# One-core hybrid decoder layer: contiguous halves for the modulation and Q/K weights, and a reordered start

## The chip, the cores and the metric

The kernel runs on one core of one Trainium2 chip. The metric is the device time of one execution, in microseconds (us). Lower is better. Everything is float32 outside; large products are split into a rounded high part and a low remainder, so that three fast passes replace one slow float32 product.

## The reference, cut to what matters

One decoder layer over 256 tokens of width 1024, with a modulation computed from a single vector `c`:

```
mod   = silu(c) @ w_ada + b_ada            # 3 x 1024
shift, scale, gate = split(mod, 3)
h     = rmsnorm(x, norm_g) * (1 + scale) + shift
proj  = h @ w_in                           # ten blocks of 1024 columns: q, k, v, ...
attn  = causal softmax attention(q, k, v) + relative-position bias
y     = two gated branches (attention, short convolution), merged
out   = rmsnorm(x + gate * (merged @ w_out), final_g)
```

With 256 tokens there is one key block, so the attention is plain causal attention with the bias `rel_bias[bucket(distance)]` for each head. This case is about what happens before and in the first projection: `silu(c)`, the two modulation columns `shift` and `scale` for each of eight 128-row slices of `h`, the normalized and transposed input, the bias table, and then `q` and `k`.

## The kernel before

The work is staged as: prologue, Q/K projection, V projection, 36 column units (convolution, gates, merges, the attention heads woven between them), output projection, tail. The order of most of the prologue is fixed by hand: `pin` keeps an instruction in program order on its engine. Every engine runs its own list in order.

**Loads.** SyncE (SP) issues nearly all loads, in the order of the code: the vector `c` into row 96 of a zeroed tile `crow` (L123), the two halves of `x` (L124, L125), the modulation weights of slice 0 in two pieces (`load_ada`, L103), the first Q/K slab in two halves (`load_slab`, L114), then the small table `oneh` for the bias (L129), then slice by slice a modulation tile (`load_wide`, L108) and a slab. Each modulation tile and each slab is 128 rows of 2048 numbers, 1 MB; every load takes 1024 of the 2048 columns, so in DRAM its rows are 4 KB long and start 8 KB apart. ScalarE (ACT) issues one load at the start, `vecs` (L122).

**Prologue.** TensorE runs four warm-up products (L231), then the broadcast of `c` over 128 partitions in two halves of 512 columns (`broadcast`, L237: a product of ones with the 97 rows of `crow`, 96 of them zero), the transposition of `vecs` between them (L249), one warm-up product, the eight transposed and normalized blocks of the first token half (`xn_trans(0, k, d0)`, L228), one warm-up, the eight of the second half, the product that picks the bias values out of `oneh` (L272), two warm-ups, and then the first Q/K slice (`passes(0)`, L221: sixteen float32 products, 32 records).

Beside it ACT squares and sums both halves of `x` (`square`, L246; the first before the sigmoid of the first half of `c`), applies the sigmoid (L242), and builds the diagonal matrices `d0`, `d1` from the reciprocal roots that GpSimd (POOL) computes (`rms_diag`). VectorE (DVE) finishes `silu(c)` (L243) and forms the modulation dots: for slice 0 four dots of 512 columns (`ada_dot`, L165), each into its own column of `parts`, which a reduction (L168) adds to the bias that POOL copied into a fifth column (L263). The first modulated slice `hfs[0]` (L275) on ACT waits for that sum, and `passes(0)` for `hfs[0]`.

**Q/K loop.** For each slice i (L286): DVE computes the modulation of the next slice in two dots of 1024 columns (`wide_dot`, L173, which start from the bias), ACT and DVE split the next slab into high and low parts (L203, L210), ACT and DVE make the next slice of `h` (L181, L191), and TensorE accumulates 16 column tiles into all eight PSUM banks (L221). After the loop comes V, whose products need nothing from the prologue but `h`.

Of the kernel before, what the change touches and what calls it, by code (L numbers as in the profile page):

```python
# [26 lines left out]
WARM = 4  # L27
WARM2 = 1
WARM3 = 1
WARM4 = 2  # L30
CROW = 96
HALF = 8
AHEAD = 3
VCUT = 640
NATIVES = [16, 2, 0, 0, 0, 0, 0, 0]
CUTS0 = (0, 2, 4)
UNITS = ([("ada", i) for i in range(KT)] + [("gate", i) for i in range(4)]
# [7 lines left out]
def layer_kernel(ctx: ExitStack, tc, x, c, vec, wp_all, slab_all, onehot, final_g, out):  # L45
# [48 lines left out]
    scs = const.tile([P, KT, 2], F32, name="scs")  # L94
    parts = const.tile([P, KT, 2, 5], F32, name="parts")
# [4 lines left out]
    def load_ada(i, cuts):  # L100
        adas[i] = big.tile([P, 2048], F32, tag=("AT", "YB", "V")[i % 3], name=f"ada{i}")
        for a, b in zip(cuts, cuts[1:]):
            pin(nc.sync.dma_start(adas[i][:, a * 512:b * 512], wp_all[UNIT["ada", i]][:, a * 512:b * 512]))  # L103

    def load_wide(i):
        adas[i] = big.tile([P, 2048], F32, tag=("AT", "YB", "V")[i % 3], name=f"ada{i}")
        for s in range(2):
            pin(nc.sync.dma_start(adas[i][:, s * D:(s + 1) * D], wp_all[UNIT["ada", i]][:, s * D:(s + 1) * D]))  # L108

    def load_slab(i, h):  # L110
        if h == 0:
            slabs[i] = raw_tile([P, NT * P], f"slab{i}")
        cols = slice(HALF * P, NT * P) if h else slice(0, HALF * P)
        pin(nc.sync.dma_start(slabs[i][:, cols], slab_all[i * P:(i + 1) * P, cols]))  # L114

    def load_ktile(i):
        load_slab(i, 0)
        if i + 1 < KT:
            load_wide(i + 1)
        load_slab(i, 1)  # L120

    pin(nc.scalar.dma_start(vecs, vec))  # L122
    pin(nc.sync.dma_start(crow[CROW:CROW + 1, :], c))  # L123
    pin(nc.sync.dma_start(xx[:, 0, :], x[0:P, :]))  # L124
    pin(nc.sync.dma_start(xx[:, 1, :], x[P:2 * P, :]))  # L125
    load_ada(0, CUTS0)
    for h in range(2):
        load_slab(0, h)
    pin(nc.sync.dma_start(oneh, onehot))  # L129
    load_wide(1)  # L130
    for i in range(1, AHEAD):
# [4 lines left out]
    nc.vector.memset(mhalf, -0.5)  # L136
    nc.vector.memset(parts[:, :, :, 2:4], 0.0)
    make_identity(nc, ident)
# [18 lines left out]

    def ada_dot(i, cuts, n):
        for a, b in zip(cuts, cuts[1:]):
            w = (b - a) * 256  # L160
            for s in range(2):
                for q in range(0, w, n):
                    k = a * 256 + q
                    src = adas[i][:, a * 512 + s * w + q:a * 512 + s * w + q + n]
                    pin(nc.vector.tensor_tensor_reduce(src, src, csb[:, k:k + n], vT[:, i:i + 1] if s else 1.0, 0.0,  # L165
                                                       ALU.mult, ALU.add, parts[:, i, s, k // n:k // n + 1]))
                    yield
        pin(nc.vector.reduce_sum(scs[:, i, :], parts[:, i], axis=mybir.AxisListType.X))  # L168

    def wide_dot(i):  # L170
        for s in range(2):
            src = adas[i][:, s * D:(s + 1) * D]
            pin(nc.vector.tensor_tensor_reduce(src, src, csb, vT[:, i:i + 1] if s else 1.0, modb[:, i, s:s + 1],  # L173
                                               ALU.mult, ALU.add, scs[:, i, s:s + 1]))

    def run(gen, n=9):
        for _ in range(n):
            next(gen, None)

# [64 lines left out]

    def square(t):
        pin(nc.scalar.activation(xx[:, 2 + t, :], xx[:, t, :], AF.Square, accum_out=ss[:, t:t + 1]))  # L246
# [12 lines left out]
    d1 = rms_diag(ss[:, 1:2], "r1")  # L259
    modb = vT[:, 8:24].rearrange("p (k s) -> p k s", s=2)  # L260
    pin(nc.gpsimd.tensor_scalar_add(modb[:, :, 1], modb[:, :, 1], 1.0))
    pin(nc.gpsimd.tensor_mul(modb[:, :, 1], modb[:, :, 1], vT[:, 0:KT]))
    pin(nc.gpsimd.tensor_copy(parts[:, :, :, 4], modb))  # L263
# [373 lines left out]


def _ada(w, cols, cuts):
    t = [w[:, c0:c0 + P].T for c0 in cols]  # L640
    return np.concatenate([h[:, a * 256:b * 256] for a, b in zip(cuts, cuts[1:]) for h in t], axis=1)


def _layout(inp):
    w_ada, w_in = inp["w_ada"][0], inp["w_in"][0]
    w_o = {"oa": inp["w_o_attn"][0], "oc": inp["w_o_conv"][0]}
    units = []
    for key in UNITS:
        blk = key[0]
        if blk == "ada":  # L650
            units.append(_ada(w_ada, [key[1] * P, D + key[1] * P], (0, 4) if key[1] else CUTS0))
        elif blk == "gate":
            units.append(_ada(w_ada, [2 * D + (2 * key[1] + d) * P for d in range(2)], (0, 4)))
# [11 lines left out]
    return {"x": inp["x"], "c": inp["c"], "vec": vec, "wp": np.stack(units), "slab": w_in[:, 0:NT * P],  # L665
            "onehot": np.concatenate([_onehot(), inp["rel_bias"]], axis=1), "final_g": inp["final_g"]}
# [17 lines left out]
```

## Time and profile before

| what | value |
|---|---|
| median of three runs | 330.81 us |
| the three runs | 330.81, 330.83, 327.39 us |
| the profiled execution's own time | 327.31 us |
| its span in the trace | 325.5 us |
| TensorE busy | 317.4 us |
| VectorE busy | 247.2 us |
| ScalarE busy | 187.8 us |
| DRAM read | 71.39 MB |

The span runs from the first to the last instruction of the trace; the execution's own time has 1.8 us more around it. Busy times are sums of instruction times; a float32 product appears as two records on TensorE. Times in the rows are microseconds from the start of the span, unless a column says ns.

### The profile page before, as it was taken

Reading aid. Unit: us, or ns where it says so; the run is one execution under the profiler, and the core shown is the slowest. Engines: PE = TensorE matmul, PEld = TensorE weight load, DVE = VectorE, ACT = ScalarE, POOL = GpSimd, SP = SyncE. Lnnn points to the kernel's source line nnn. Section 1 sums busy time; section 2 is a strip of 40 time slices with the busy share of each in tenths; the row PEclk is TensorE's granted clock in tenths of the full one; section 3 lists DMA queues with packets and bytes.
Section 4 is the critical chain, followed back from the end, with each engine's and each line's share of the span. In section 5 each row is a group of like instructions: output and inputs, shape, how many; then the busy total and the mean of one; then the engine's idle time right before and its main releaser. Section 6 shows DMA issues by size and latency. Waiting matters only on the chain.

```text
span 325.5 us, 4909 instructions
## 1 busy us (share of the span) xinstructions
PE 317.4 (98%) x1894; PEld 280.5 (86%) x1894; DVE 247.2 (76%) x406; ACT 187.8 (58%) x304; POOL 6.4 (2%) x18
## 2 busy tenths in 40 slices
PE   8899999999999999999999999999999999999992
PEld 5799999988888888888888888888888888888892
DVE  1889985874469777796857998999755566888764
ACT  6255646745498586775757656766565636453430
POOL 2300000000000000000000000000000000000010
PEclk9999999999999999999999999999999999999999
DMA  6999999985474345434533559559974656400003
GB/s 223 388 408 410 406 413 416 393 322 222 156 250 139 131 186 197 136 130 158 200 159 131 224 204 375 222 155 408 366 283 172 265 178 221 157 3 0 0 2 129
DMA packets 14175, 72.77 MB, mean 224 GB/s; under 512 B 1503, under 2 KB 2887, under 8 KB 8008
## 3 DMA queue, kind: packets, MB, share of 16 engines
q1 hardware_dynamic: 12562, 70.45, 57.1%
q10 hardware_dynamic: 1558, 2.00, 1.8%
q8 instruction: 15, 0.25, 0.3%
q14 instruction: 8, 0.07, 0.1%
q0 software_dynamic: 32, 0.01, 0.0%
HBM read 71.39 MB, written 1.06 MB: 223 GB/s over the span
## 4 chain that ended last, share of the span: by engine, by line
PE 92%; DMA 3%; issue 1%; SPq 1%; ACT 0%; DVE 0%; POOL 0%; POOLq 0%; ACTq 0%
PE acc L221 15%; PE aoa L349 5%; PE aoc L349 5%; PE acx L349 5%; PE acc L349 5%; PE acb L349 5%; PE ama L349 5%; PE amc L349 5%; PE aga L349 5%; PE agc L349 5%; DMA oneh<-in_onehot_dram 3%; PE aoa L350 2%; PE aoc L350 2%; PE acx L350 2%; PE acb L350 2%; PE acc L350 2%
## 5 line engine op out<-in xcount | busy, mean ns | idle before, releaser
L173 DVE CUSTOM_DVE_ANT_0 ada<-ada,csb,vT 128x1024 f32<-128x1024 f32 x14 | 17.8, 1309 | 0.0
L416 DVE CUSTOM_DVE_ANT_0 L<-pS,BI 128x128 f32<-128x128 f32 x8 | 2.3, 292 | 12.2 <-PE pS L413 12.2
L221 PE MATMUL acc<-hf,slab 128*128 128x256 f32 x36 | 8.1, 379 | 0.0
L581 POOL TENSOR_TENSOR rf<-ms,mhalf 128x1 f32<-128x1 f32 x2 | 1.7, 866 | 303.8 <-DVE ms L606 300.2
L221 PEld LDWEIGHTS acc<-hf,slab 128*128 128x128 f32 x36 | 6.7, 190 | 0.8
L563 ACT ACTIVATE SQ<-TT 128x512 f32<-128x512 f32 x3 | 1.9, 627 | 7.6 <-DVE TT L558 7.6
L386 DVE CUSTOM_DVE_ANT_0 gate<-gate,csb,vT 128x512 f32<-128x512 f32 x8 | 6.0, 746 | 0.2 <-DMA gate<-in_wp_dram 0.2
L349 PE MATMUL acc<-H,cc2h 128*128 128x512 f32 x16 | 5.8, 404 | 0.0
L349 PE MATMUL aoa<-GA,oa0h 128*128 128x512 f32 x16 | 5.8, 404 | 0.0
L349 PE MATMUL aoa<-GA,oa1h 128*128 128x512 f32 x16 | 5.7, 399 | 0.0
L349 PE MATMUL aoc<-GC,oc2h 128*128 128x512 f32 x16 | 5.7, 399 | 0.0
L349 PE MATMUL aoc<-GC,oc1h 128*128 128x512 f32 x16 | 5.7, 399 | 0.0
L349 PE MATMUL aoa<-GA,oa3h 128*128 128x512 f32 x16 | 5.7, 399 | 0.0
L349 PE MATMUL acx<-H,cx0h 128*128 128x512 f32 x16 | 5.7, 398 | 0.0
L349 PE MATMUL acb<-H,cb1h 128*128 128x512 f32 x16 | 5.7, 398 | 0.0
L349 PE MATMUL aoc<-GC,oc0h 128*128 128x512 f32 x16 | 5.7, 398 | 0.0
L349 PE MATMUL aoa<-GA,oa2h 128*128 128x512 f32 x16 | 5.7, 398 | 0.0
L349 PE MATMUL aoc<-GC,oc3h 128*128 128x512 f32 x16 | 5.7, 398 | 0.0
L349 PE MATMUL acc<-H,cc0h 128*128 128x512 f32 x16 | 5.7, 398 | 0.0
L349 PE MATMUL acx<-H,cx1h 128*128 128x512 f32 x16 | 5.7, 398 | 0.0
L349 PE MATMUL acx<-H,cx3h 128*128 128x512 f32 x16 | 5.7, 398 | 0.0
L349 PE MATMUL acb<-H,cb3h 128*128 128x512 f32 x16 | 5.7, 398 | 0.0
(465 smaller groups left out, 1215.8 us busy)
## 6 DMA issues: line engine op xcount, KB each, us to landing
ada<-in_wp_dram SPq DMA_DIRECT2D x16, 512.0 KB, 9.9
slab<-in_slab_dram SPq DMA_DIRECT2D x16, 512.0 KB, 10.2
wv<-in_wp_dram SPq DMA_DIRECT2D x4, 1024.0 KB, 11.3
wcc<-in_wp_dram SPq DMA_DIRECT2D x4, 1024.0 KB, 7.8
wcx<-in_wp_dram SPq DMA_DIRECT2D x4, 1024.0 KB, 4.7
wcb<-in_wp_dram SPq DMA_DIRECT2D x4, 1024.0 KB, 5.0
wgc<-in_wp_dram SPq DMA_DIRECT2D x4, 1024.0 KB, 4.8
wga<-in_wp_dram SPq DMA_DIRECT2D x4, 1024.0 KB, 4.8
```

What stands on the lines that cost most here:

```text
L173: pin(nc.vector.tensor_tensor_reduce(src, src, csb, vT[:, i:i + 1] if s else 1.0, modb[:, i, s:s + 1], ALU.mult, ALU.add, scs[:, i, s:s + 1]))
L221: pin(nc.tensor.matmul(acc[j // 2][:, (j % 2) * S:(j % 2 + 1) * S], w[i][:, j * P:(j + 1) * P], x, start=(i == 0 and j // 2 not in opened) ...
L349: nc.tensor.matmul(a, hi[:, k, cols], rhs[:, k, :], start=(k == 0), stop=False)
L350: nc.tensor.matmul(a[:, S:], lo[:, k, cols], rhs[:, k, 0:S], start=False, stop=(k == KT - 1))
L386: nc.vector.tensor_tensor_reduce(src, src, csb[:, q * 512:(q + 1) * 512], 1.0, 0.0 if q else vT[:, 24 + b:25 + b], ALU.mult, ALU.add, gpar ...
L416: nc.vector.tensor_tensor_reduce(L[:, 0:P], pS[:, 0:P], BI[:, h, 0:P][:, ::-1], 1.0, -3.0e38, ALU.add, ALU.max, mx[:, 0:1])
L563: nc.scalar.activation(SQ[:, t, 0:w], TT[:, t, cols], AF.Square, accum_out=s8[:, slot:slot + 1])
L581: nc.gpsimd.tensor_tensor(r, ms, mhalf, op=ALU.pow)
```

## The change

1. **Layout.** On the host, each modulation tile is stored as two contiguous halves of 128 x 1024 (`_halves`), and the slabs as sixteen such blocks. A load now reads 512 KB that lie together, 128 rows of 4 KB one after the other. What lands in which tile is the same.
2. **Bias table.** `oneh` is loaded on ACT's queue right after `vecs`, not on SP's queue behind the first slab. Its product moves on TensorE from behind the transposes to right behind the second broadcast.
3. **c.** It goes into row 127 of `crow`; the broadcast has 128 rows instead of 97.
4. **First square.** The sum of squares of the first token half moves from ACT to DVE, as a product with a running sum over 1024 columns, ahead of the first `silu` product. On ACT the square of the second half now stands ahead of `d0`.
5. **Dots.** The dots of slice 0 start from the bias (or from the first half's sum), so `parts`, its memset, the reduction and POOL's copy go. The scaled bias is written into a tile of its own, `msc`, by POOL ahead of `r1`.
6. **Warm-ups.** Three instead of one ahead of the first transposes, one behind the last instead of one between the two groups, and the two behind the bias product go.

```diff
-WARM2 = 1
+WARM2 = 3
 WARM3 = 1
-WARM4 = 2
-CROW = 96
+CROW = P - 1
...
+    def load_ada(i):
         adas[i] = big.tile([P, 2048], F32, tag=("AT", "YB", "V")[i % 3], name=f"ada{i}")
+        unit = wp_all[UNIT["ada", i]]
         for s in range(2):
-            pin(nc.sync.dma_start(adas[i][:, s * D:(s + 1) * D], wp_all[UNIT["ada", i]][:, s * D:(s + 1) * D]))
+            src = bass.AP(tensor=unit.tensor, offset=unit.offset + s * P * D, ap=[[D, P], [1, D]])
+            pin(nc.sync.dma_start(adas[i][:, s * D:(s + 1) * D], src))
...
-        pin(nc.sync.dma_start(slabs[i][:, cols], slab_all[i * P:(i + 1) * P, cols]))
+        pin(nc.sync.dma_start(slabs[i][:, cols], slab_all[(2 * i + h) * P:(2 * i + h + 1) * P, :]))
...
     pin(nc.scalar.dma_start(vecs, vec))
+    pin(nc.scalar.dma_start(oneh, onehot))
...
-    pin(nc.sync.dma_start(oneh, onehot))
...
+    def first_dots(a):
+        cols = slice(a * 512, (a + 1) * 512)
+        for s in range(2):
+            src = adas[0][:, a * D + s * 512:a * D + (s + 1) * 512]
+            pin(nc.vector.tensor_tensor_reduce(src, src, csb[:, cols], vT[:, 0:1] if s else 1.0,
+                                               half[:, s:s + 1] if a else bias(0, s), ALU.mult, ALU.add,
+                                               scs[:, 0, s:s + 1] if a else half[:, s:s + 1]))
...
     broadcast(1)
-    square(0)
+    pb = pv[0:NH, P:512]
+    pin(nc.tensor.matmul(pb[:, 126:], oneh[:, 3 * P:], oneh[:, 126:3 * P], start=True, stop=True))
+    pin(nc.vector.tensor_tensor_reduce(xx[:, 2, :], xx[:, 0, :], xx[:, 0, :], 1.0, 0.0, ALU.mult, ALU.add, ss[:, 0:1]))
     silu_part(0)
     pin(nc.scalar.activation(vT, pv[:, 0:56], AF.Copy))
+    pin(nc.scalar.activation(xx[:, 3, :], xx[:, 1, :], AF.Square, accum_out=ss[:, 1:2]))
     d0 = rms_diag(ss[:, 0:1], "r0")
-    square(1)
-    dot = ada_dot(0, CUTS0, 512)
-    run(dot, 2)
+    modb = vT[:, 8:24].rearrange("p (k s) -> p k s", s=2)
+    pin(nc.gpsimd.tensor_scalar_add(msc, modb[:, :, 1], 1.0))
+    pin(nc.gpsimd.tensor_mul(msc, msc, vT[:, 0:KT]))
+    first_dots(0)
     silu_part(1)
     d1 = rms_diag(ss[:, 1:2], "r1")
...
-    run(dot)
+    first_dots(1)
     warm(WARM2)
-    for k in range(KT):
-        xn_trans(0, k, d0)
+    for t, d in enumerate((d0, d1)):
+        for k in range(KT):
+            xn_trans(t, k, d)
     warm(WARM3)
-    for k in range(KT):
-        xn_trans(1, k, d1)
-    pb = pv[0:NH, P:512]
-    pin(nc.tensor.matmul(pb[:, 126:], oneh[:, 3 * P:], oneh[:, 126:3 * P], start=True, stop=True))
-    warm(WARM4)
...
+def _halves(w):
+    return w.reshape(P, 2, D).transpose(1, 0, 2).reshape(P, 2048)
...
-    "slab": w_in[:, 0:NT * P],
+    "slab": w_in[:, 0:NT * P].reshape(KT, P, 2, D).transpose(0, 2, 1, 3).reshape(2 * KT * P, D),
```

## Rows read from the trace of the kernel before

**Rows 1.** The page: span, and busy time of each engine with its share and instructions.

```profile
span 325.5 us, 4909 instructions
...
PE 317.4 (98%) x1894; PEld 280.5 (86%) x1894; DVE 247.2 (76%) x406; ACT 187.8 (58%) x304; POOL 6.4 (2%) x18
```

**Rows 2.** Chain that ended last, in order: start us, us, what; prologue and Q/K.

```profile
4.06 9.44 DMA oneh<-in_onehot_dram
13.54 0.60 PE pv L272 x2
14.14 0.64 PE wt L147 x4
14.78 47.36 PE acc L221 x366
```

**Rows 3.** Windows: stretch, length, busy (records) by engine, granted clock, DMA share, GB/s.

```profile
3.00:4.80 1.80, 1.80 (x4) 0.29 (x3) 0.00 (x0) 0.49 (x1) 0.00 (x0) 1.00 1.03 412
5.00:10.00 5.00, 5.00 (x18) 3.92 (x18) 1.40 (x4) 3.38 (x9) 2.57 (x7) 1.00 0.86 276
...
15.00:62.00 47.00, 47.00 (x366) 46.09 (x366) 39.53 (x55) 26.70 (x35) 0.63 (x1) 1.00 1.02 409
62.00:313.00 251.00, 251.00 (x1426) 218.60 (x1425) 194.56 (x316) 152.12 (x251) 0.00 (x0) 1.00 0.52 191
```

**Rows 4.** Timeline of TensorE: start us, us, instruction, idle before and releaser.

```profile
2.92 1.92 PE L237 MATMUL pc<-crow,ones 97*128 97x512 f32 x2
...
5.04 2.07 PE L237 MATMUL pc<-crow,ones 97*128 97x512 f32 x2
6.91 0.63 PE L147 MATMUL wt<-ones 128*128 128x128 f32 x2
7.34 3.31 PE L228 MATMUL px<-r0d,xx 128*128 128x128 f32 x16
...
10.70 1.95 PE L228 MATMUL px<-r1d,xx 128*128 128x128 f32 x16
13.54 0.60 PE L272 MATMUL pv<-oneh 32*8 32x258 f32 x2 [0.89 <-DMA oneh<-in_onehot_dram]
...
14.62 7.07 PE L221 MATMUL acc<-hf,slab 128*128 128x256 f32 x32
21.34 0.83 PE L221 MATMUL acc<-H,slab1h 128*128 128x256 f32 x4
```

**Rows 5.** Tile px: ns min/median/max of one record, first and last start.

```profile
L228 PE MATMUL px<-r0d,xx x16: 275/421/421, 7.3 to 10.4; 128*128 128x128 f32 x16
...
L228 PE MATMUL px<-r1d,xx x16: 275/275/275, 10.7 to 12.4; 128*128 128x128 f32 x16
```

**Rows 6.** Timeline of the other engines beside the prologue.

```profile
0.73 0.63 ACTq L122 DMA_DIRECT2D vecs<-in_vec_dram  x1
...
4.31 1.06 ACT L246 ACTIVATE xx<-xx 128x1024 f32<-128x1024 f32 x1 [1.42 <-DMA xx<-in_x_dram]
...
6.41 0.40 ACT L155 ACTIVATE r0d<-ident,r0r 128x128 f32<-128x128 f32 x1 [0.36 <-POOL r0r L153]
...
9.28 0.69 DVE L165 CUSTOM_DVE_ANT_0 ada<-ada,csb 128x512 f32<-128x512 f32 x1 [2.62 <-DMA ada<-in_wp_dram]
...
10.57 0.68 DVE L243 TENSOR_TENSOR csb<-csb,pc 128x512 f32<-128x512 f32 x1
...
11.91 0.75 DVE L165 CUSTOM_DVE_ANT_0 ada<-ada,csb,vT 128x512 f32<-128x512 f32 x1
...
12.77 0.16 DVE L168 TENSOR_REDUCE scs<-parts 128x2 f32<-128x10 f32 x1
...
13.03 0.56 ACT L275 ACTIVATE hf<-px,scs 128x256 f32<-128x256 f32 x1 [3.83 <-DVE scs L168]
...
14.97 1.28 DVE L173 CUSTOM_DVE_ANT_0 ada<-ada,csb,vT 128x1024 f32<-128x1024 f32 x1
...
18.16 0.59 ACT L181 ACTIVATE H<-xnT,scs 128x256 fp32r<-128x256 f32 x1
```

More of the change, by code (lines that the diff above doesn't have):

```diff
@@ L35 @@
 NATIVES = [16, 2, 0, 0, 0, 0, 0, 0]
-CUTS0 = (0, 2, 4)
 UNITS = ([("ada", i) for i in range(KT)] + [("gate", i) for i in range(4)]
@@ L94, in layer_kernel @@
     scs = const.tile([P, KT, 2], F32, name="scs")
-    parts = const.tile([P, KT, 2, 5], F32, name="parts")
+    half = const.tile([P, 2], F32, name="half")
+    msc = const.tile([P, KT], F32, name="msc")
     gcol = const.tile([P, KT], F32, name="gcol")
@@ L98, in layer_kernel @@
     adas, slabs, hfs, his, los = {}, {}, {}, {}, {}
-    def load_ada(i, cuts):
+    def load_ada(i):
         adas[i] = big.tile([P, 2048], F32, tag=("AT", "YB", "V")[i % 3], name=f"ada{i}")
[L102 to L106, printed above, removed]
+        unit = wp_all[UNIT["ada", i]]
         for s in range(2):
-            pin(nc.sync.dma_start(adas[i][:, s * D:(s + 1) * D], wp_all[UNIT["ada", i]][:, s * D:(s + 1) * D]))
+            src = bass.AP(tensor=unit.tensor, offset=unit.offset + s * P * D, ap=[[D, P], [1, D]])
+            pin(nc.sync.dma_start(adas[i][:, s * D:(s + 1) * D], src))
     def load_slab(i, h):
@@ L118, in load_ktile @@
         if i + 1 < KT:
-            load_wide(i + 1)
+            load_ada(i + 1)
         load_slab(i, 1)
     pin(nc.scalar.dma_start(vecs, vec))
+    pin(nc.scalar.dma_start(oneh, onehot))
     pin(nc.sync.dma_start(crow[CROW:CROW + 1, :], c))
@@ L125, in layer_kernel @@
     pin(nc.sync.dma_start(xx[:, 1, :], x[P:2 * P, :]))
-    load_ada(0, CUTS0)
+    load_ada(0)
     for h in range(2):
         load_slab(0, h)
-    pin(nc.sync.dma_start(oneh, onehot))
-    load_wide(1)
+    load_ada(1)
     for i in range(1, AHEAD):
@@ L136, in layer_kernel @@
     nc.vector.memset(mhalf, -0.5)
-    nc.vector.memset(parts[:, :, :, 2:4], 0.0)
     make_identity(nc, ident)
@@ L156, in rms_diag, with bias @@
         return d
[L158 to L168, printed above, removed]
+    def bias(i, s):
+        return msc[:, i:i + 1] if s else vT[:, 8 + 2 * i:9 + 2 * i]
+    def first_dots(a):
[5 more added lines that the diff above has]
+                                               scs[:, 0, s:s + 1] if a else half[:, s:s + 1]))
     def wide_dot(i):
@@ L172, in wide_dot @@
             src = adas[i][:, s * D:(s + 1) * D]
-            pin(nc.vector.tensor_tensor_reduce(src, src, csb, vT[:, i:i + 1] if s else 1.0, modb[:, i, s:s + 1],
+            pin(nc.vector.tensor_tensor_reduce(src, src, csb, vT[:, i:i + 1] if s else 1.0, bias(i, s),
                                                ALU.mult, ALU.add, scs[:, i, s:s + 1]))
-    def run(gen, n=9):
-        for _ in range(n):
-            next(gen, None)
     def modulated(i, dst):
@@ L243, in silu_part @@
         pin(nc.vector.tensor_mul(csb[:, cols], csb[:, cols], pc[n]))
-    def square(t):
-        pin(nc.scalar.activation(xx[:, 2 + t, :], xx[:, t, :], AF.Square, accum_out=ss[:, t:t + 1]))
     broadcast(0)
@@ L250, in layer_kernel @@
     broadcast(1)
-    square(0)
+    pb = pv[0:NH, P:512]
+    pin(nc.tensor.matmul(pb[:, 126:], oneh[:, 3 * P:], oneh[:, 126:3 * P], start=True, stop=True))
+    pin(nc.vector.tensor_tensor_reduce(xx[:, 2, :], xx[:, 0, :], xx[:, 0, :], 1.0, 0.0, ALU.mult, ALU.add, ss[:, 0:1]))
     silu_part(0)
     pin(nc.scalar.activation(vT, pv[:, 0:56], AF.Copy))
+    pin(nc.scalar.activation(xx[:, 3, :], xx[:, 1, :], AF.Square, accum_out=ss[:, 1:2]))
     d0 = rms_diag(ss[:, 0:1], "r0")
-    square(1)
-    dot = ada_dot(0, CUTS0, 512)
-    run(dot, 2)
+    modb = vT[:, 8:24].rearrange("p (k s) -> p k s", s=2)
+    pin(nc.gpsimd.tensor_scalar_add(msc, modb[:, :, 1], 1.0))
+    pin(nc.gpsimd.tensor_mul(msc, msc, vT[:, 0:KT]))
+    first_dots(0)
     silu_part(1)
     d1 = rms_diag(ss[:, 1:2], "r1")
[L260 to L263, printed above, removed]
-    run(dot)
+    first_dots(1)
     warm(WARM2)
-    for k in range(KT):
-        xn_trans(0, k, d0)
+    for t, d in enumerate((d0, d1)):
+        for k in range(KT):
+            xn_trans(t, k, d)
     warm(WARM3)
-    for k in range(KT):
-        xn_trans(1, k, d1)
-    pb = pv[0:NH, P:512]
-    pin(nc.tensor.matmul(pb[:, 126:], oneh[:, 3 * P:], oneh[:, 126:3 * P], start=True, stop=True))
-    warm(WARM4)
     hfs[0] = tp.tile([P, S], F32, tag="low", name="hf0", bufs=4)
@@ L636, in _rows @@
     return w[kh * 512:(kh + 1) * 512, c0:c0 + 512].reshape(4, P, 512).transpose(1, 0, 2).reshape(P, 2048)
+def _halves(w):
+    return w.reshape(P, 2, D).transpose(1, 0, 2).reshape(P, 2048)
 def _ada(w, cols, cuts):
     t = [w[:, c0:c0 + P].T for c0 in cols]
-    return np.concatenate([h[:, a * 256:b * 256] for a, b in zip(cuts, cuts[1:]) for h in t], axis=1)
+    return np.concatenate([h[:, a * 512:b * 512] for a, b in zip(cuts, cuts[1:]) for h in t], axis=1)
 def _layout(inp):
@@ L650, in _layout @@
         if blk == "ada":
-            units.append(_ada(w_ada, [key[1] * P, D + key[1] * P], (0, 4) if key[1] else CUTS0))
+            units.append(_halves(_ada(w_ada, [key[1] * P, D + key[1] * P], (0, 2) if key[1] else (0, 1, 2))))
         elif blk == "gate":
-            units.append(_ada(w_ada, [2 * D + (2 * key[1] + d) * P for d in range(2)], (0, 4)))
+            units.append(_ada(w_ada, [2 * D + (2 * key[1] + d) * P for d in range(2)], (0, 2)))
         elif blk == "v":
@@ L664, in _layout @@
                           inp["conv_w"].reshape(3 * KT, P)])
-    return {"x": inp["x"], "c": inp["c"], "vec": vec, "wp": np.stack(units), "slab": w_in[:, 0:NT * P],
+    return {"x": inp["x"], "c": inp["c"], "vec": vec, "wp": np.stack(units),
+            "slab": w_in[:, 0:NT * P].reshape(KT, P, 2, D).transpose(0, 2, 1, 3).reshape(2 * KT * P, D),
             "onehot": np.concatenate([_onehot(), inp["rel_bias"]], axis=1), "final_g": inp["final_g"]}
```

## The prediction

> **What bounds the kernel now.** I read the totals first, then the chain of waits, then windows by stage, and last the timeline of the first 22 us. The totals say TensorE is busy for 317.4 of 325.5 us [rows 1], but busy is not yet bound. The windows settle it: from 15 to 62 us and from 62 to 313 us TensorE is busy in every microsecond, 47.00 of 47.00 and 251.00 of 251.00, and the granted clock is 1.00 [rows 3]. No engine and no load interrupts it there. So an edit counts only by how much earlier the first Q/K product starts, or by what it does to the last 12 us, and the change doesn't touch those.
>
> What sets that start is in the chain: the load of the bias table, issued at 4.06 and landed 9.44 us later, then the bias product (0.60), two warm-ups (0.64), then 47.36 us of Q/K products without a break [rows 2]. The table is small, but it stands in SP's queue behind both halves of x, the first modulation tile and the first slab. TensorE had finished the transposes at about 12.65 (10.70 + 1.95) and stood idle 0.89 us before it [rows 4].
>
> One release behind that wait is another: the first modulated slice on ACT starts at 13.03, released by the reduction on DVE, and ends at 13.59 [rows 6]. So freeing the table alone can't bring the first product from 14.62 below about 13.6.
>
> **The change part by part.**
>
> *Bias table and its product.* From behind the transposes go the wait (0.89), the product (start 13.54) and two warm-ups; from 12.65 to the Q/K start at 14.62 there are 1.97 us to win at most [rows 4]. The second issue on ACT costs about what the first did, 0.63 us [rows 6]; ACT's first real work starts at 4.31, so that is hidden behind the load of x. On the DMA engines the table now runs beside x. SP's queue loses one issue; every load behind it moves up by the table's few KB. I take zero for both.
>
> The product now stands behind the second broadcast, ahead of the transposes. Does the table make it? The broadcast ends near 7.1 (5.04 + 2.07) [rows 4]; a load issued near 1.4 and not queued behind 3 MB has over 5 us. I take no wait; if it were late, all transposes would queue behind it.
>
> *Price of the moved TensorE work.* The transposes show two paces for the same shape: a record takes 421 ns until about 10.3 and 275 ns after it [rows 5], and sixteen take 3.31 us before and 1.95 us after, 0.207 and 0.122 us each [rows 4]. The granted-clock column says 1.00 throughout [rows 3], so only the record lengths show it: the engine works at the lower of its levels (1.2 GHz) until 10.3, then at the higher (2.4 GHz), having run without a gap since 2.92. The bias product used to run at the higher level and now runs at the lower. Its price there isn't in the trace; the floor is 0.60 [rows 2], the ceiling half of a broadcast of 512 columns, about 1.0 (2.07 / 2) [rows 4]. I take 1.0, because it stands beside the broadcasts. The two extra warm-ups take 0.43 each from start to start (6.91 to 7.34): 0.86. So the transposes start at 7.34 + 1.86 = 9.20. Until 10.3, five records run at 0.207; the other 27 at 0.122 make 3.3 us: they end at 13.6. One warm-up behind them takes about 0.3 (half of 0.64 [rows 2]). TensorE is free at **13.9**. So half of what the table's wait gives back is paid for ahead of the transposes.
>
> *First square on DVE.* DVE has the price at this shape: 1.28 us [rows 6]. From x's landing at 4.31 it ends near 5.7, a little before the old start of the first silu product. On ACT the 1.06 us in front of the sigmoid goes, but the second square now stands ahead of the first diagonal, which before was ready at 6.81 (6.41 + 0.40): with the sigmoid, a copy and 1.06 for the square it is ready near 7.4 [rows 6]. TensorE wants it at 9.20, so the bias product and the warm-ups hide it; without them it would cost about 0.1. The second diagonal comes earlier than before. POOL's two small steps for the scaled bias move ahead of the second root and hide under the same cover.
>
> *Dots from the bias.* The chain on DVE is two dots, the second silu product, two dots: from 9.28 to 12.66 (11.91 + 0.75). The reduction of 0.16 at its end goes [rows 6]. The first slice is then ready at about 13.4 instead of 13.59. This is under the 13.9 of TensorE, so it gives nothing by itself; it would be next in line.
>
> *c in row 127.* The columns streamed stay 512, and memsets keep their width. I take zero; below zero only if it changes when TensorE's level rises, see the rivals.
>
> *Contiguous halves.* In the Q/K stage the loads, rows 8 KB apart, already run at 409 GB/s, as the contiguous x does at 412 [rows 3]: no gain there. Between 5 and 10 us, however, they moved only 276 GB/s. If that dip is due to the 8 KB step, contiguity returns (409 - 276) x 5 us = 0.67 MB, or 1.6 us of landing time, and the dots start that much earlier. If not, nothing. Either way TensorE at 13.9 hides it: zero in the sum, 1.6 as the other end. The Trainium skill, page "DMA: Bandwidth & Descriptors", section "Latency and other measured facts", says that rows at certain large power-of-two steps lower the rate and that laying tiles out contiguously restores it; its steps are far larger, and the 409 GB/s here speak against applying it.
>
> *Does a gain at the start survive?* The second slice's first product ran at 21.34; its high part of h was ready at 18.75 (18.16 + 0.59) [rows 4, 6]. That is 2.6 us of slack, and behind it a window with no idle TensorE [rows 3].
>
> **Sum.** 14.62 - 13.9 = 0.7 us. Against the profiled execution's own 327.31 (span 325.5, 1.8 around it) this makes **326.6**. How that stands to the median: the three runs shown are 327.39, 330.81 and 330.83; the profiled execution belongs with the lowest, and no row shows where the other 3.4 us are, which are more than any term here. I give the median of the changed kernel 0.55 to lie with the lower value and 0.45 with the upper, some 3.5 higher (330.1).
>
> **Rivals.**
>
> *A. The lower level ends sooner and the loads land sooner.* If 128 rows instead of 97 or the longer unbroken run raise TensorE's level near 7 us, the bias product takes 0.60, three warm-ups 0.9, 32 records 3.9, one warm-up 0.3: free at 12.7. Alone, the start falls to the slice at 13.4, a gain of 1.2; with loads 1.6 us earlier the slice is ready by 11.8 and the start is 12.7: a gain of 1.9, **325.4**. For: both edits touch just these. Against: the level stayed low through the gap-free broadcasts [rows 4]. Chance 0.20.
>
> *B. The change doesn't do what it says:* the start stays, because a small cost is missed (the slice, a landing slab). **327.3**. For: two chains within 0.5 us of each other. Chance 0.15.
>
> *C. Slower: the level rises later.* If it rose only after the transposes, they would all run at 0.207: 9.20 + 6.6 = 15.8, with the warm-up 16.2, or 1.6 us later than now: **328.9**. Each further microsecond at the lower level costs half a microsecond; the point from which it is slower at all is a rise behind 12. The rise is seen once, at 10.3 [rows 5], so its place is not known to be fixed. Chance 0.10, and 0.04 that it is over 1%. The Trainium skill, page "TensorE: Matmul & The Clock Gate", Part 1, says the moment of the rise differs from run to run of one kernel; by that rule A and C can both occur in runs of this kernel; no row here can show it.
>
> **How the numbers follow.** Forecast 0.55, A 0.20, B 0.15, C 0.10. The forecast's own range is 326.0 to 327.1 (bias product at its floor of 0.60; a level rise half a microsecond later). About 1% is what a measurement of this kernel can tell from no change: 327.5 and below against 330.81. Faster by more needs the lower value of the runs (0.55) and forecast, A or B (0.9): 0.49. Slower by more: 0.04. The rest, 0.47, is within 1%, mostly the same mechanism at the upper value. The range goes from 325.0 (A with a little more) to 330.4 (the forecast at the upper value, 330.1); outside lie B and C at the upper value and the long form of C, under 0.2.
>
> **What would show it.** Right: the bias product near 7 us with no wait for its load; transposes without a break from about 9.2 to 13.6; the first Q/K product near 13.9; the first slice ready before it; the chain of waits leading back through TensorE to the broadcast, with no load in it; a full TensorE from there to 313. Wrong: transposes that start near 8.4 at 275 ns (A), that are 421 ns to the end (C), or a wait of TensorE for the first slice (DVE is the bound, and then the landing of the first modulation tile, 9.28 now, is the number to read). A loss in the Q/K loop, an idle TensorE behind 15 us, would contradict the slack that I read.

## The result, and the profile after

The changed kernel takes 325.76 us (median of 20 executions, 325.19 to 327.13), the kernel before 327.38 in the same job (20 executions, 326.26 to 330.87): ratio 0.9928, 95% interval 0.9901 to 0.9955. That is a gain of 0.7%, inside the 1% band and inside the range. The ratio is one of means; the medians give 0.9951, since seven of the 20 executions of the kernel before took 329.5 us or more. The likeliest value was 326.6. The three runs known at the forecast held two of those high ones, so the median before is now 3.4 us lower than the one shown.

The profiled execution took 327.01 us. It is one of three of the 20 between 326.9 and 327.1; the other 17 took 325.9 or less. Its page and its chain of waits (start us, us, what):

```profile
span 325.2 us, 4906 instructions
...
PE 317.1 (98%) x1894; PEld 279.5 (86%) x1894; DVE 248.3 (76%) x406; ACT 186.8 (57%) x302; POOL 6.0 (2%) x17
```

```profile
1.99 5.79 DMA ada<-in_wp_dram
7.95 0.75 DVE ada L160
...
11.67 0.57 ACT hf L258
12.29 47.63 PE acc L211 x366
```

The table has left the chain [rows 2]. It now leads from the landing of the first modulation half through the dots and the first slice to the Q/K product, which starts at 12.29 instead of 14.62, 2.33 us earlier. TensorE's timeline in the prologue (start us, us, instruction, idle before and releaser):

```profile
2.91 1.81 PE L227 MATMUL pc<-crow,ones 128*128 128x512 f32 x2
...
4.84 1.12 PE L227 MATMUL pc<-crow,ones 128*128 128x512 f32 x2
5.90 0.60 PE L239 MATMUL pv<-oneh 32*8 32x258 f32 x2
6.43 0.94 PE L142 MATMUL wt<-ones 128*128 128x128 f32 x6
8.13 2.05 PE L218 MATMUL px<-r0d,xx 128*128 128x128 f32 x16 [0.77 <-ACT r0d L150]
10.02 1.95 PE L218 MATMUL px<-r1d,xx 128*128 128x128 f32 x16
11.80 0.39 PE L142 MATMUL wt<-ones 128*128 128x128 f32 x2
12.29 7.17 PE L211 MATMUL acc<-hf,slab 128*128 128x256 f32 x32
```

The second broadcast takes 1.12 us where it took 2.07, and the first sixteen transposes 2.05 where they took 3.31 [rows 4]: TensorE reached its higher level (2.4 GHz) near 4.6 us, still in the first broadcast (1.81 where it took 1.92), instead of 10.3. Then it waits 0.77 us for the first diagonal. Why that is late stands with the other engines:

```profile
6.54 0.22 ACT L242 ACTIVATE vT<-pv 128x56 f32<-128x56 f32 x1 [1.18 <-PE pv L239]
6.65 1.05 ACT L243 ACTIVATE xx<-xx 128x1024 f32<-128x1024 f32 x1
...
7.69 0.39 ACT L150 ACTIVATE r0d<-ident,r0r 128x128 f32<-128x128 f32 x1
...
7.95 0.75 DVE L160 CUSTOM_DVE_ANT_0 ada<-ada,csb,vT 128x512 f32<-128x512 f32 x1 [1.38 <-ACT xx L243]
...
10.75 0.81 DVE L160 CUSTOM_DVE_ANT_0 ada<-ada,csb,half 128x512 f32<-128x512 f32 x1
...
11.67 0.56 ACT L258 ACTIVATE hf<-px,scs 128x256 f32<-128x256 f32 x1 [2.10 <-DVE scs L160]
```

The copy of vT waits for the bias product, which writes the same PSUM tile and is issued ahead of it; the second square and the diagonal queue behind the copy. The dots start 1.33 us earlier [rows 6]. The windows (stretch, length, busy by engine, clock, DMA share, GB/s):

```profile
5.00:10.00 5.00, 4.23 (x26) 2.85 (x27) 3.62 (x8) 2.78 (x7) 2.35 (x6) 1.00 1.02 410
...
15.00:62.00 47.00, 47.00 (x365) 46.01 (x364) 40.23 (x54) 28.93 (x37) 0.00 (x0) 1.00 1.03 408
62.00:313.00 251.00, 251.00 (x1416) 217.98 (x1416) 192.46 (x314) 150.03 (x249) 0.00 (x0) 1.00 0.52 189
```

From 5 to 10 us the loads move 410 GB/s, not 276 [rows 3]. Behind 15 us TensorE is again busy throughout. And yet the start is 2.33 us earlier and the span only 0.3 us shorter. The same full busy column holds 1416 records where it held 1426 [rows 3]: TensorE was as busy, and slower. Two tiles of the unit stage show it, the first `ga` and the last `mc` unit (ns min/median/max of a record, first and last start), before:

```profile
L349 PE MATMUL aga<-H,ga0h x16: 392/394/395, 185.2 to 190.3; 128*128 128x512 f32 x16
...
L349 PE MATMUL amc<-H,mc3h x16: 392/394/395, 246.2 to 251.4; 128*128 128x512 f32 x16
```

and after:

```profile
L332 PE MATMUL aga<-H,ga0h x16: 395/398/403, 183.6 to 188.9; 128*128 128x512 f32 x16
...
L332 PE MATMUL amc<-H,mc3h x16: 395/399/403, 245.8 to 251.1; 128*128 128x512 f32 x16
```

Eleven units lie between the two: 61.0 / 11 = 5.55 us a unit before, 62.2 / 11 = 5.65 after. At `ga0` the changed kernel leads by 1.6 us, at `mc3` by 0.4. The Trainium skill, page "Trainium Kernel Development and Optimization", section "Performance Expectations", warns that matmul busy time is a bad measure of how close a kernel is to its limit, because matmuls are pipelined; the trace agrees, 251.00 busy in 251 us on both sides.

So there are two paces, and this one execution had the worse. The eleven profiles of kernels in which every unit alternates its products of 512 and 256 columns sort by it. In the table, "start" is the first Q/K product, "rest" is span minus start:

| profile | rows in the broadcast | second broadcast | start | span | rest |
|---|---|---|---|---|---|
| before | 97 | 2.07 | 14.62 | 325.5 | 310.9 |
| after | 128 | 1.12 | 12.29 | 325.2 | 312.9 |
| e1_row96 | 97 | 2.07 | 15.48 | 326.4 | 310.9 |
| e2_strided | 128 | 1.32 | 12.91 | 323.9 | 311.0 |
| e3_table_late | 128 | 1.21 | 13.26 | 324.2 | 310.9 |
| e4_before_row127 | 128 | 1.12 | 15.43 | 327.9 | 312.5 |
| e5_before_halves | 97 | 1.12 | 13.79 | 326.6 | 312.8 |
| e6_before_table | 97 | 2.07 | 15.02 | 325.9 | 310.9 |
| e8_prologue | 128 | 1.84 | 12.94 | 323.8 | 310.9 |
| e11_square_act | 128 | 1.41 | 12.98 | 323.9 | 310.9 |
| e12_start | 128 | 1.34 | 11.83 | 322.8 | 311.0 |

The rest is 310.9 to 311.0 in eight of eleven and 312.8 or 312.9 in two; e4 is explained below. The prologue thus acts on the start alone, and the pace adds 2.0 us or nothing. An estimate from the medians (1.8 us around the span, rest 310.9) gives a typical start of 13.1 for the changed kernel (325.76) and 14.7 for the one before (327.38): 1.6 us.

The pace is not one of a whole execution. In both slow profiles, that of the changed kernel and e5, the units fall behind the others from `cb0` on (6.48 us from its start to that of `cc1`, 6.37 in the other nine), and the gate and merge units stay slow to the last `mc`; the output-gate units behind them take 5.65 us in all eleven. Both have the shortest second broadcast of the table, 1.12, but e4 has it too and kept the faster pace, with a fall of the clock in between. Whether the early rise has to do with the pace was not tested.

### The profile page after: what moved, and what is told of

Same layout as the page of the kernel before. It is cut to its first block, busy times and chain, and to the rows that moved or that the text cites. A ratio compares the mean times of both kernels' runs of the same rounds, so it can differ in the third digit from the quotient of the medians.

```text
span 325.2 us, 4906 instructions
## 1 busy us (share of the span) xinstructions
PE 317.1 (98%) x1894; PEld 279.5 (86%) x1894; DVE 248.3 (76%) x406; ACT 186.8 (57%) x302; POOL 6.0 (2%) x17
## 3 DMA queue, kind: packets, MB, share of 16 engines
q10 hardware_dynamic: 1606, 2.05, 2.0%
HBM read 71.39 MB, written 1.06 MB: 223 GB/s over the span
## 4 chain that ended last, share of the span: by engine, by line
PE 94%; DMA 2%; DVE 1%; ACT 0%; SPq 0%; issue 0%; POOLq 0%; DVEq 0%; ACTq 0%
PE acc L211 15%; PE amc L332 5%; PE aoc L332 5%; PE aoa L332 5%; PE ama L332 5%; PE agc L332 5%; PE aga L332 5%; PE acb L332 5%; PE acc L332 5%; PE acx L332 5%; PE acb L333 2%; PE acc L333 2%; PE aga L333 2%; PE agc L333 2%; PE aoc L333 2%; PE amc L333 2%
## 5 line engine op out<-in xcount | busy, mean ns | idle before, releaser
L167 DVE CUSTOM_DVE_ANT_0 ada<-ada,csb,msc 128x1024 f32<-128x1024 f32 x7 | 9.4, 1341 | 0.0
L167 DVE CUSTOM_DVE_ANT_0 ada<-ada,csb,vT 128x1024 f32<-128x1024 f32 x7 | 9.0, 1279 | 0.0
L332 PE MATMUL acc<-H,cc3h 128*128 128x512 f32 x16 | 5.8, 404 | 0.0
L332 PE MATMUL agc<-H,gc0h 128*128 128x512 f32 x16 | 5.8, 404 | 0.0
L332 PE MATMUL agc<-H,gc1h 128*128 128x512 f32 x16 | 5.8, 404 | 0.0
L332 PE MATMUL acc<-H,cc1h 128*128 128x512 f32 x16 | 5.8, 404 | 0.0
L332 PE MATMUL agc<-H,gc3h 128*128 128x512 f32 x16 | 5.7, 399 | 0.0
L332 PE MATMUL aga<-H,ga2h 128*128 128x512 f32 x16 | 5.7, 399 | 0.0
L332 PE MATMUL ama<-H,ma1h 128*128 128x512 f32 x16 | 5.7, 399 | 0.0
L332 PE MATMUL amc<-H,mc0h 128*128 128x512 f32 x16 | 5.7, 399 | 0.0
## 6 DMA issues: line engine op xcount, KB each, us to landing
wv<-in_wp_dram SPq DMA_DIRECT2D x4, 1024.0 KB, 11.3
```

Source lines behind the costliest of these rows:

```text
L332: nc.tensor.matmul(a, hi[:, k, cols], rhs[:, k, :], start=(k == 0), stop=False)
```

## The experiments

Ratios are to the kernel before in the same job, where its median lay between 327.4 and 328.2. The changed kernel itself ran in the first job only, so small differences of times to its 325.76 are not clear.

**e1_row96**: the changed kernel with c back in row 96.

```diff
-CROW = P - 1
+CROW = 96
```

> The changed kernel with c back in row 96, so that the broadcasts have 97 rows. Theory (full rows raise TensorE's level): the second broadcast is slow again (near 2.07 us instead of 1.12), the level rises during the transposes, records of the first transposes are 421 ns, and the first Q/K product starts near 13.9 instead of 12.29; time 1.0 to 1.6 us above the changed kernel, near 327. Rival (the rise moves by itself from execution to execution, or comes from the bias product and the denser warm-ups): second broadcast near 1.1 us or transposes at 275 ns, start at 12.3, time unchanged at 325.8.

327.70 us, ratio to before 0.9982 (0.9942 to 1.0021). TensorE's timeline:

```profile
5.04 2.07 PE L227 MATMUL pc<-crow,ones 97*128 97x512 f32 x2
7.04 1.02 PE L239 MATMUL pv<-oneh 32*8 32x258 f32 x2
8.00 1.65 PE L142 MATMUL wt<-ones 128*128 128x128 f32 x6
9.70 3.78 PE L218 MATMUL px<-r0d,xx 128*128 128x128 f32 x16
13.27 2.15 PE L218 MATMUL px<-r1d,xx 128*128 128x128 f32 x16
...
15.48 1.89 PE L211 MATMUL acc<-hf,slab 128*128 128x256 f32 x8
```

The bias product at the lower level costs 1.02 us, as the forecast priced it (1.0). The level rises only near 13.7, in the second group of transposes, and the start is 0.86 us later than before, which is close to rival C. Two of the ten executions took 325.0, though, which fits an early rise with 97 rows, as e5 has it in its profile.

**e4_before_row127**: the kernel before with 128 rows and nothing else.

```diff
-CROW = 96
+CROW = P - 1
```

> The kernel before with nothing but c in row 127 (128-row broadcasts). Theory (full rows raise the level): second broadcast near 1.1 us, all transposes at 275 ns; but the bias table still lands near 13.5, so the first Q/K product stays at 14.6 and the time at 327.4. Rival (rows don't matter): the second broadcast stays near 2.07 us and the first transposes at 421 ns. A gain of over 0.5 us in the time would contradict both.

329.26 us, ratio 1.007 (1.0038 to 1.0102): slower, which neither theory had. The level rises early, the transposes end near 11.4, and TensorE then stands idle for the table:

```profile
14.21 0.60 PE L272 MATMUL pv<-oneh 32*8 32x258 f32 x2 [2.77 <-DMA oneh<-in_onehot_dram]
14.73 0.90 PE L147 MATMUL wt<-ones 128*128 128x128 f32 x4
15.43 8.61 PE L221 MATMUL acc<-hf,slab 128*128 128x256 f32 x32
```

The windows behind it (the last columns are granted clock, DMA share, GB/s) show the clock falling:

```profile
15.00:17.00 2.00, 2.00 (x8) 1.73 (x8) 2.00 (x5) 0.21 (x1) 0.77 (x1) 0.53 1.03 416
17.00:19.00 2.00, 2.00 (x7) 1.59 (x7) 1.29 (x3) 1.15 (x2) 0.00 (x0) 0.62 1.02 410
19.00:21.00 2.00, 2.00 (x11) 1.77 (x10) 2.00 (x3) 0.89 (x2) 0.00 (x0) 1.00 1.02 406
```

Behind the idle time the clock fell back to the lower level in the first Q/K slice, which took 8.61 us instead of 7.07. The 1.54 us are its larger rest of 312.5. Here the granted-clock column shows the lower level; in the prologue it reads 1.00 throughout, and the level has to be read from the lengths of the records.

**e2_strided**: the changed kernel with the old layout in DRAM.

```diff
-            src = bass.AP(tensor=unit.tensor, offset=unit.offset + s * P * D, ap=[[D, P], [1, D]])
-            pin(nc.sync.dma_start(adas[i][:, s * D:(s + 1) * D], src))
+            pin(nc.sync.dma_start(adas[i][:, s * D:(s + 1) * D], unit[:, s * D:(s + 1) * D]))
...
-slab_all[(2 * i + h) * P:(2 * i + h + 1) * P, :]
+slab_all[i * P:(i + 1) * P, cols]
```

> The changed kernel with modulation tiles and slabs in the old layout, rows 8 KB apart. Theory (contiguity took the dip out of the early loads): 5 to 10 us move near 280 GB/s instead of 410, the first dot starts near 9.3 instead of 7.95, the first slice 1.3 us later, first Q/K product near 13.6; time 1.0 to 1.6 us above the changed kernel. Rival (the dip came from the table in SP's queue or from something else that the change moved): near 400 GB/s, first dot at 8.0, no change in time.

326.18 us, ratio 0.9966 (0.993 to 1.0003). Windows, then VectorE's first dot:

```profile
5.00:10.00 5.00, 4.23 (x24) 2.81 (x24) 3.09 (x8) 2.89 (x7) 1.96 (x6) 1.00 0.96 348
```

```profile
8.57 0.75 DVE L159 CUSTOM_DVE_ANT_0 ada<-ada,csb,vT 128x512 f32<-128x512 f32 x1 [1.91 <-ACT r0d L149]
```

In between: 348 GB/s instead of 280 or 400, and the first dot at 8.57 instead of 9.3 or 8.0. The start is 12.91, no later than the typical 13.1 of the changed kernel, and no loss of time is shown.

**e5_before_halves**: the kernel before with contiguous halves alone (the layout edits of the change, nothing else).

```diff
+            src = bass.AP(tensor=unit.tensor, offset=unit.offset + s * P * D, ap=[[D, P], [1, D]])
...
-slab_all[i * P:(i + 1) * P, cols]
+slab_all[(2 * i + h) * P:(2 * i + h + 1) * P, :]
```

> The kernel before with the contiguous halves alone. Theory: 5 to 10 us move near 400 GB/s, the first dot starts near 8.0 instead of 9.28, and the bias table, still behind 3 MB in SP's queue, lands near 12.0 instead of 13.5, so the first Q/K product starts 1.0 to 1.5 us earlier, limited by the transposes that end near 12.65; time near 326.2. Rival (the dip is not the layout): dot at 9.3, table at 13.5, no change.

326.58 us, ratio 0.9975 (0.9948 to 1.0003). 360 GB/s from 5 to 10 us, first dot at 8.59, table landed at 12.7, start 13.79: less than the theory gave, and more than nothing. The profiled execution is the slowest of the ten (328.52; the others 326.07 to 326.70) and the one with the slower pace. Here the level rose early with 97 rows:

```profile
4.95 1.12 PE L241 MATMUL pc<-crow,ones 97*128 97x512 f32 x2
...
12.72 0.60 PE L276 MATMUL pv<-oneh 32*8 32x258 f32 x2 [1.36 <-DMA oneh<-in_onehot_dram]
```

**e3_table_late**: the changed kernel with the table's load behind the first slab and its product behind the transposes.

```diff
-    pin(nc.scalar.dma_start(oneh, onehot))
...
         load_slab(0, h)
+    pin(nc.sync.dma_start(oneh, onehot))
```

> The changed kernel with the bias table back in SP's queue behind the first slab and its product behind the transposes; everything else as changed. Theory (the table is the part that frees the start once the rest is early): TensorE waits for the table, which lands near 12.0 to 12.7 thanks to the contiguous loads; the first Q/K product starts 13.0 to 13.7 instead of 12.29, 0.7 to 1.4 us lost, time near 326.8. Rival (the loads are now early enough that the table no longer matters): table landed by 11.8, start at 12.4, time unchanged.

326.08 us, ratio 0.9945 (0.9901 to 0.999). The start is 13.26, as the theory had it, but the 326.8 expected did not come. TensorE waits again, though briefly:

```profile
12.41 0.60 PE L255 MATMUL pv<-oneh 32*8 32x258 f32 x2 [0.99 <-DMA oneh<-in_onehot_dram]
...
13.26 2.97 PE L211 MATMUL acc<-hf,slab 128*128 128x256 f32 x13
```

**e6_before_table**: the kernel before with the table loaded on ScalarE's queue.

```diff
     pin(nc.scalar.dma_start(vecs, vec))
+    pin(nc.scalar.dma_start(oneh, onehot))
...
-    pin(nc.sync.dma_start(oneh, onehot))
```

> The kernel before with the bias table alone loaded early, on ScalarE's queue; its product stays behind the transposes. Theory: no wait of TensorE for the table; the first Q/K product starts near 13.7, held by the first slice (13.59 before), 0.9 us earlier; the profile's span is its start plus 310.9 or 312.9, as in all profiles so far; time near 326.4, and the group of executions at 330.8 is gone, because it needs the long idle TensorE in front of the table after an early rise of its level (a level drop in the first Q/K slice, as in the profile of e4_before_row127). Rival for the last point: the group at 330.8 stays, its cause is elsewhere.

326.43 us, ratio 0.9962 (0.9928 to 0.9995): the median is the 326.4 expected. The profiled execution (327.68) is one of the three slower ones: the wait for the table is gone, but the level rose only near 12, so that TensorE was free later, not earlier, with the start at 15.02. None of the ten executions is above 328.5; of 29 of the kernel before in that job twelve are above 329.0, four of them above 330.8. Their mean granted clock is 0.988 to 0.993, that of the ten here 0.995 to 0.999; the profiled execution of e4, with the fall in view, has 0.992. So the slower executions of the kernel before, those above 330.8 most clearly, ran part of their time at a lower clock, and that fits the reading that they had the idle TensorE of e4. No profile of such an execution was had, and e9, with the table as late, has none below 0.994, so it stays a reading.

**e7_grouped, e9_before_grouped**: the changed kernel and the one before, with all products of 512 columns of a unit half ahead of those of 256.

```diff
                 nc.tensor.matmul(a, hi[:, k, cols], rhs[:, k, :], start=(k == 0), stop=False)
+            for k in range(KT):
                 nc.tensor.matmul(a[:, S:], lo[:, k, cols], rhs[:, k, 0:S], start=False, stop=(k == KT - 1))
```

> The changed kernel; in each of the 36 column units the eight products of 512 columns of one output half run first and the eight of 256 columns after them, instead of alternating. In the two profiled executions the alternating stream runs at one of two paces, 5.43 or 5.53 us from the first to the last record of a unit, and in the changed kernel's profile fourteen units in a row (gates and merges) kept the slower one, where the kernel before kept the faster. Theory (this pace ate 2.0 of the 2.3 us won at the start): the grouped order has one pace, near 16 x (0.227 + 0.120) = 5.55 us a unit from start to start, against 5.66 for a slow one and 5.55 for a fast one; the profile from the first unit to the output projection gets 2 to 3 us shorter, and the time falls from 325.8 to 323 to 324.5 with little spread. Rival (the loss comes from elsewhere, loads or VectorE behind the units): units stay at their times, no change in time.

> The kernel before with the same grouping. Theory: its executions, now split between 327 and 330.8, fall on one value near 325.5 to 326.5, and the difference to the grouped changed kernel shows the start alone, 1.5 to 2.3 us. Rival: the split stays, since it comes from the start.

328.19 us (327.66 to 328.54) and 329.75 us (328.99 to 330.60); ratios 0.9998 (0.9957 to 1.0038) and 1.006 (1.0024 to 1.0095). Grouping made both kernels slower, so the times that I expected failed; that the grouped order has one pace and shows the start alone held. Tiles of e7, then its window:

```profile
L332 PE MATMUL aga<-H,ga0h x16: 389/391/398, 186.3 to 190.7; 128*128 128x512 f32 x16
...
L332 PE MATMUL amc<-H,mc3h x16: 389/392/398, 247.8 to 252.2; 128*128 128x512 f32 x16
```

```profile
62.00:313.00 251.00, 248.72 (x1413) 218.05 (x1412) 190.91 (x315) 149.39 (x249) 0.00 (x0) 1.00 0.52 189
```

There is one pace, 61.5 / 11 = 5.59 us a unit, between the two; and 2.28 us of idle TensorE appear where attention heads are woven between the units (a transposition there waits for the exponential on ScalarE). Both profiles have the same rest, 313.5 us (326.6 - 13.06 and 327.8 - 14.27), and the executions spread 0.9 and 1.6 us, where the 20 of the kernel before spread 4.6. With the pace fixed, the change is worth 329.75 - 328.19 = 1.56 us by the medians; in the two profiles it is 1.21, all of it at the start.

The prologue of e7 is that of the changed kernel, so it is a second look at it, with the level rising later (near 6.9):

```profile
5.04 1.97 PE L227 MATMUL pc<-crow,ones 128*128 128x512 f32 x2
6.94 0.60 PE L239 MATMUL pv<-oneh 32*8 32x258 f32 x2
7.57 0.22 ACT L242 ACTIVATE vT<-pv 128x56 f32<-128x56 f32 x1 [2.11 <-PE pv L239]
...
11.95 0.56 ACT L258 ACTIVATE hf<-px,scs 128x256 f32<-128x256 f32 x1 [1.38 <-DVE scs L160]
12.84 0.39 PE L142 MATMUL wt<-ones 128*128 128x128 f32 x2
13.06 3.19 PE L211 MATMUL acc<-hf,slab 128*128 128x256 f32 x14
```

The first slice is ready at 12.51, and the Q/K product starts only at 13.06, behind the transposes and the last warm-up. Here it is not the dots that hold the start, but the bias product, the copy of vT, the second square, the first diagonal and the transposes, one behind the other. And 13.06 is the typical start estimated above.

**e11_square_act**: the changed kernel with the first square back on ScalarE.

```diff
-    pin(nc.vector.tensor_tensor_reduce(xx[:, 2, :], xx[:, 0, :], xx[:, 0, :], 1.0, 0.0, ALU.mult, ALU.add, ss[:, 0:1]))
+    pin(nc.scalar.activation(xx[:, 2, :], xx[:, 0, :], AF.Square, accum_out=ss[:, 0:1]))
...
-    pin(nc.scalar.activation(xx[:, 3, :], xx[:, 1, :], AF.Square, accum_out=ss[:, 1:2]))
     d0 = rms_diag(ss[:, 0:1], "r0")
+    pin(nc.scalar.activation(xx[:, 3, :], xx[:, 1, :], AF.Square, accum_out=ss[:, 1:2]))
```

> The changed kernel with the first square back on ScalarE, ahead of the sigmoid, and the second behind the first diagonal, as in the kernel before. Theory (the move of the square bought nothing, since the diagonal is late because of the second square and the wait of vT's copy): first diagonal ready at 7.4 to 7.7 instead of 8.08, start of the first Q/K product within 0.3 us of 12.3 to 12.9, time unchanged at 325.8. Rival (the square on ScalarE delays the sigmoid and with it the dots): first slice and start over 0.5 us later, time near 326.5.

325.84 us, ratio 0.9939 (0.9907 to 0.9972): no difference to the changed kernel. The first diagonal is in time (ready at 7.51), the second is now what TensorE waits for, and the start is 12.98:

```profile
10.87 2.05 PE L218 MATMUL px<-r1d,xx 128*128 128x128 f32 x16 [1.24 <-ACT r1d L150]
```

**e8_prologue**: bias product issued behind the copy of vT, second silu ahead of the second square, first diagonal on VectorE.

```diff
-    pb = pv[0:NH, P:512]
-    pin(nc.tensor.matmul(pb[:, 126:], oneh[:, 3 * P:], oneh[:, 126:3 * P], start=True, stop=True))
...
     pin(nc.scalar.activation(vT, pv[:, 0:56], AF.Copy))
+    pb = pv[0:NH, P:512]
+    pin(nc.tensor.matmul(pb[:, 126:], oneh[:, 3 * P:], oneh[:, 126:3 * P], start=True, stop=True))
+    silu_part(1)
     pin(nc.scalar.activation(xx[:, 3, :], xx[:, 1, :], AF.Square, accum_out=ss[:, 1:2]))
-    d0 = rms_diag(ss[:, 0:1], "r0")
+    d0 = rms_diag(ss[:, 0:1], "r0", True)
...
-    silu_part(1)
```

> The changed kernel with the bias product issued behind the copy of vT (the copy waited for it until 6.54), the second silu part ahead of the second square and of the first dots, and the first diagonal built on VectorE. Theory (the start is set by the dots of slice 0, and TensorE's wait of 0.77 us for the diagonal is not on that chain): the diagonal is ready near 7.4 and TensorE no longer waits for it; the dots run without the silu product among them, the first slice is ready near 11.5 instead of 12.24, and the first Q/K product starts 0.6 to 0.8 us earlier, near 11.6; time 0 to 0.8 us lower (the pace of the units may hide it). Rival (TensorE's own work sets the start): nothing moves, or the landing of the second modulation half (near 9) holds the dots and the start stays at 12.3.

325.68 us, ratio 0.9935 (0.9905 to 0.9966): no gain. The copy of vT no longer waits for the bias product:

```profile
5.36 0.21 ACT L243 ACTIVATE vT<-pv 128x56 f32<-128x56 f32 x1
```

The dots end at 11.3 instead of 11.56, but the silu now delays the square (7.41 instead of 6.65) and with it the second diagonal, and the transposes end only near 12.9; the start is 12.94.

**e12_start**: as e8, but with the second silu behind the square and ahead of the dots, and one warm-up instead of three. **e10_best**: e12 with the grouped order in the eight `oa` and `oc` units alone. The edits against the changed kernel, without those shown for e8 and e7:

```diff
-WARM2 = 3
+WARM2 = 1
...
-    first_dots(0)
     silu_part(1)
+    first_dots(0)
```

```diff
-        ya = unit(("oa", j), GA, tmp("cc", f"ya{j}"))
+        ya = unit(("oa", j), GA, tmp("cc", f"ya{j}"), True)
...
-        yc = unit(("oc", j), GC, tmp("cx", f"yc{j}"))
+        yc = unit(("oc", j), GC, tmp("cx", f"yc{j}"), True)
```

> The changed kernel with the bias product issued behind the copy of vT, the first diagonal built on VectorE, the second silu product ahead of the first dots, and one warm-up instead of three ahead of the transposes. Theory (in the changed kernel the wait for the diagonal and the dots both hold the start): TensorE waits less than 0.3 us for the first diagonal, the first Q/K product starts near 12.0 (12.3 to 13.1 in the profiles of the changed layout with 128 rows), time 0.5 to 1.0 us under the changed kernel's 325.8. Rival (fewer warm-ups or an earlier gap keep TensorE at its lower level longer, or the second diagonal comes later): start at 12.8 or later, no gain.

> The changed kernel with the start of e12_start, and with the grouped order in the eight units of the two output gates (oa, oc) alone, which run at 5.65 us a unit in every profile so far, against 5.585 for the grouped order. Theory: 8 x 0.07 = 0.5 us shorter there, with no idle TensorE since no attention head is woven in, and a start near 12.0; time near 324.6 to 325.0, under both kernels. Rival (grouping brings gaps, as it did in the attention stage): no gain over e12_start.

e12: 324.89 us, ratio 0.9906 (0.9875 to 0.9937), 0.95 us under e11 in the same job. Transposes start at 7.16, without a wait, and the start is 11.83, held by the first slice:

```profile
7.16 1.96 PE L221 MATMUL px<-r0d,xx 128*128 128x128 f32 x16
8.96 1.95 PE L221 MATMUL px<-r1d,xx 128*128 128x128 f32 x16
...
11.83 4.37 PE L214 MATMUL acc<-hf,slab 128*128 128x256 f32 x19 [0.69 <-ACT hf L261]
```

e10: 324.23 us, ratio 0.9895 (0.9852 to 0.9938), start 12.08 and rest 322.5 - 12.08 = 310.4, the 0.5 us expected. It is the fastest version tried, under both kernels.

## Why the prediction was right or wrong

The direction and the range were right; the likeliest mechanism was not. What happened at the start is most of rival A, with 0.20: its sign, transposes near 8.4 at 275 ns, is there (8.13). The measured 325.76 lies below the forecast's own 326.0 to 327.1, in the part of the range that was there for A. The doubt about the median came out at the lower value: the high executions known then were a minority, seven of 20, and the changed kernel has none. The outcome within 1% had 0.47, a gain beyond it 0.49, both against 330.81.

- **TensorE stays at its lower level until 10.3**: this step failed. I took the moment of the rise in one profile as fixed and priced the moved work against it. By the lengths of the records, the rise comes between about 4.6 and 6.9 us in all nine profiles with 128 rows (second broadcast 1.12 to 1.97 us, all first transposes near 2.0); with 97 rows it comes near 4.9 in one profile and between 9.0 and 13.7 in the other four. The term of 1.86 us for the bias product and two more warm-ups measured about 1.1 at the higher level (bias product 0.53 from start to start, two warm-ups 0.6). In e1, where the level did stay low, the product cost what I had (1.02) and the warm-ups more: three took 1.70 from start to start, and the transposes began at 9.70, not 9.20. The 0.207 for a record at the lower level was a little low as well, since the last of those sixteen already ran faster [rows 5]; in e1 sixteen took 3.57 from start to start, 0.223 each.
- **c in row 127 at zero, unless it moves the level**: it does, and it is the part whose removal costs most (325.76 to 327.70; ratios 0.9928 and 0.9982, their intervals just overlap). Alone it is a loss (e4): it lengthens the idle wait for the table, and the clock falls behind it. The dots' start from the bias and the warm-ups were not taken out by themselves, so what they give is not shown.
- **Bias table**: right, no wait, and the load landed in time. Put back, the median is 326.08, only 0.3 us above, which the intervals don't tell from none: earlier loads bring the table 1.1 us sooner (12.41 instead of 13.54).
- **Contiguous halves hidden behind TensorE**: wrong in consequence, since TensorE was early and the dots became a bound. The dip is not the layout alone. With the table in SP's queue, 5 to 10 us moved 276, 304 and 329 GB/s with rows 8 KB apart (the kernel before, e4, e9) and 360 and 377 contiguous (e5, e3); with the table early, 348 and 386 (e2, e6) and 359 to 410. So each of the two shows where the other has not been changed, and with the table early the layouts can't be told apart. These are a few profiles each, and the size of the two shares stays open. The Trainium skill, page "DMA: Bandwidth & Descriptors", section "Latency and other measured facts", advises contiguous tiles against large row steps; that is neither borne out nor refuted here: in the Q/K stage both layouts run at 407 to 410.
- **First square on DVE**: price right (1.23), cover wrong. The first diagonal ready near 7.4 needs a second square that starts near 5.9 (7.4 - 0.40 - 1.06); the copy of vT ahead of it waited for the bias product until 6.54, and the diagonal was ready at 8.08. I had not looked for a wait between two users of one PSUM tile; e8, with the product behind the copy, has the copy at 5.36. And TensorE wanted the diagonal near 7.4, not at 9.20. e11 shows no gain from the move.
- **Dots**: "next in line" was right for the profiled execution and for e12, where they hold the start. In e7, with the same prologue, the transposes do, so the two chains are about equally long.
- **A gain at the start survives**: right in the mean (1.56 with one pace, 1.6 from the medians), wrong for a single execution, in which 2.0 us went to the pace. I read a full busy column as a fixed rate.
- **Rival C's rule**, that the moment of the rise differs between executions (the Trainium skill, page "TensorE: Matmul & The Clock Gate", Part 1): the trace agrees; with the same prologue it is near 4.6 in the changed kernel and 6.9 in e7, near 10.3 in the kernel before and 9.0 in e9.

## What to carry to other kernels

A prologue is a set of chains of nearly equal length: a part that shortens one (128 rows) can lose alone and be the best part once the others are short, so undo parts from the full change as well as adding them singly. Before you cost a moved instruction, look at what else uses its PSUM tile, since a product issued ahead of a copy makes the copy wait. And where one engine is busy all the time, compare the start times of the same tile in both traces: busy share can't show a change of pace.

## What the runs showed of the hardware

- The alternating stream of 512- and 256-column products has two paces, 5.55 and 5.65 us for a unit of 32, at the same clock of 1.00. The gate and merge units kept the slower one in two of eleven profiles, at a cost of 2.0 us over the kernel, and the output-gate units had it in all. What decides it was not found. Grouping by width gives 5.59.
- TensorE's level rose sooner with 128-row broadcasts than with 97-row ones in which 96 and 127 rows alike are zero: before 7 us in nine of nine profiles against one of five.
- 2.77 us of idle TensorE were followed by a fall to the lower level (granted clock 0.53 and 0.62 in the next two stretches); 1.36 us in e5 were not.
